# A fused add and GELU bound by its DMA queue: which load goes out first

## Chip, cores and metric

One core of a Trainium2 chip. The metric is the device time of one execution in microseconds (us); lower is better. Before: 120.17 us, median of 3 executions (120.11 to 120.28).

## The reference

```python
def setup_inputs():
    batch, dim = 1024, 4096
    return {"x": randn(batch, dim) as float32, "y": randn(batch, dim) as float32}

def reference(x, y):
    z = x + y
    return 0.5 * z * (1 + tanh(sqrt(2 / pi) * (z + 0.044715 * z ** 3)))
```

Two inputs of 16.8 MB are read and one output of 16.8 MB is written. Each byte crosses the memory once, 50.33 MB in all.

## The kernel before

A partition holds 32768 columns (8 whole rows). x is loaded straight into the tile of the sum, in two loads of 64 KB per partition. y comes in four loads of 32 KB per partition and has two buffers. The sum is made in chunks of 2048 columns by GpSimd or VectorE. ScalarE takes the absolute value and then the GELU of its negative, and VectorE finishes with max(z, 0) plus that.

```python
    YS = 8192
    xloads = [16384, 16384]
    yloads = [8192, 8192, 8192, 8192]
    FIRST = 8
    stores = [16384, 10240, 6144]
    by_dve = {0: 0, 2: 0, 4: 2, 6: 4, 8: 8, 12: 10}
    # ... pools: the tile of the sum once, y twice, PSUM work tiles twice ...

    sp = []
    for i, (a, b) in enumerate(xr):
        sp += [(load_x, i)] + [(load_y, j) for j, (c, _) in enumerate(yr) if a <= c < b]
    sp += [(store, i) for i in range(len(stores))]
    # ... VectorE: for each chunk c: the adds listed for c in by_dve, then end(c) ...
    # ... a manual schedule: each engine runs its list in order ...

    begin_early(nc, 2)    # the first two loads go ahead of the barrier at which the engines meet on entry
    wait_late(nc)
```

All loads and stores are issued by one engine (SP) onto one queue: x0, y0, y1, x1, y2, y3, then three stores. y2 must wait until y0's buffer is free, and the first store is held back until chunk 8 is half finished.

Of the kernel before, what the change touches and what calls it, by code (L numbers as in the profile page):

```python
# [66 lines left out]
def kernel(  # L67
# [33 lines left out]
    def ranges(sizes):  # L101
        ends = [sum(sizes[: i + 1]) for i in range(len(sizes))]
        assert ends[-1] == TOT
        return [(e - f, e) for e, f in zip(ends, sizes)]

    xr, yr, sr, cr = (ranges(r) for r in (xloads, yloads, stores, [CH] * (TOT // CH)))
# [63 lines left out]
            ends.setdefault(c, ins.ins)  # L170


    sp = []
    for i, (a, b) in enumerate(xr):
        sp += [(load_x, i)] + [(load_y, j) for j, (c, _) in enumerate(yr) if a <= c < b]
    sp += [(store, i) for i in range(len(stores))]
    pool = [(add, c) for c in range(C) if c not in by_dve]
    dve, acts = [], []
# [69 lines left out]
```

## Time and profile before

| | before |
|---|---|
| median | 120.17 us |
| span in the profile | 118.8 us |
| DMA queue busy | 98.5% |
| VectorE, ScalarE, GpSimd busy | 50%, 51%, 47% |
| first adds begin | 31.70 us |
| first store issued | 77.86 us |

Read the DMA share first: with the engines at 98.5%, only the moments when they have nothing to do can be gained. Those lie at the start and the end of the span. The lines themselves are in the prediction below; in them DVE is VectorE, ACT ScalarE, POOL GpSimd, and SPq the instructions by which SP issues transfers.

### The profile page before, as it was taken

How to read it: one execution, taken by the hardware profiler on the slowest of the kernel's cores; microseconds unless marked ns; L12 is line 12 of the kernel's file. 1: busy time of each engine (PE TensorE's matmuls, PEld its weight loads, DVE VectorE, ACT ScalarE, POOL GpSimd, SP SyncE). 2: the span in 40 equal slices, each digit the busy share in tenths (PEclk: the TensorE clock that was granted, in tenths of full speed). 3: DMA queues.
4: the chain of work that ended last, by engine and by line, in shares of the span. 5: the costliest groups of instructions: out<-in, count | busy, mean ns of one | idle time of the engine just before them, and what ended most of it. 6: DMA issues, size and time to landing. Idle time of an engine off the chain costs nothing.

```text
span 118.8 us, 160 instructions
## 1 busy us (share of the span) xinstructions
DVE 59.8 (50%) x24; ACT 60.8 (51%) x34; POOL 55.5 (47%) x14
## 2 busy tenths in 40 slices
DVE  0000000000399999699994595257999457742000
ACT  5000000000057989999369804797798999940000
POOL 0000000000399999998000029999999999200000
DMA  9899988989999988998899999998899889999895
GB/s 353 353 419 596 397 353 364 497 375 463 419 430 452 530 353 375 640 397 353 353 463 419 452 430 397 474 541 353 375 640 397 353 353 441 441 441 441 381 422 257
DMA packets 1296, 50.33 MB, mean 424 GB/s; under 512 B 144, under 2 KB 144, under 8 KB 144
## 3 DMA queue, kind: packets, MB, share of 16 engines
q1 hardware_dynamic: 1296, 50.33, 98.5%
HBM read 33.55 MB, written 16.78 MB: 424 GB/s over the span
## 4 chain that ended last, share of the span: by engine, by line
DMA 48%; POOL 33%; POOLq 4%; ACT 3%; DVE 2%; issue 0%; SPq 0%; DVEq 0%
DMA y<-in_y_dram 48%; POOL z L149 33%; POOLq L215 4%; DVE z L166 2%; ACT w L154 2%; ACT w L157 2%; SPq L125 0%; POOLq L149 0%; DVEq L166 0%
## 5 line engine op out<-in xcount | busy, mean ns | idle before, releaser
L149 POOL TENSOR_TENSOR z<-z,y 128x2048 f32<-128x2048 f32 x10 | 55.3, 5560 | 45.9 <-DMA y<-in_y_dram 45.9
L154 ACT ACTIVATE w<-z 128x2048 f32<-128x2048 f32 x16 | 30.1, 1880 | 42.8 <-DVE z L149 36.3
L166 DVE SCALAR_TENSOR_TENSOR z<-z,w 128x2048 f32<-128x2048 f32 (+1 forms) x17 | 36.3, 2156 | 16.0 <-ACT w L157 16.0
L149 DVE TENSOR_TENSOR z<-z,y 128x2048 f32<-128x2048 f32 x6 | 24.0, 4009 | 30.6 <-DMA y<-in_y_dram 30.6
L157 ACT ACTIVATE w<-w 128x2048 f32<-128x2048 f32 x16 | 29.8, 1862 | 0.5
L200 ACT ACT_TABLE_LOAD x1 | 1.3, 1283 | 1.3 <-PEq L232 1.3
L199 DVE MEMSET one<- 128x1 f32 x1 | 0.1, 59 | 1.3 <-PEq L232 1.3
L200 ACT ACTIVATE one<-one 128x1 f32<-128x1 f32 x1 | 0.2, 203 | 0.0
L232 POOL MEMSET const-float32-0.0<- 128x1 f32 x1 | 0.1, 99 | 0.2 <-issue 0.2
L232 POOL MEMSET const-bfloat16-1.0<- 128x1 bf16 x1 | 0.1, 102 | 0.0
L232 POOL MEMSET const-uint8-127<- 128x1 uint8 x1 | 0.1, 102 | 0.0
L232 POOL MEMSET const-float32-1.0<- 128x1 f32 x1 | 0.1, 99 | 0.0
## 6 DMA issues: line engine op xcount, KB each, us to landing
y<-in_y_dram SPq DMA_DIRECT2D x4, 4096.0 KB, 28.3
out_dram<-z SPq DMA_DIRECT2D x1, 5120.0 KB, 14.9
out_dram<-z SPq DMA_DIRECT2D x1, 3072.0 KB, 10.9
z<-in_x_dram SPq DMA_DIRECT2D x2, 40.5
out_dram<-z SPq DMA_DIRECT2D x1, 21.6
```

Of the source, the lines that this page charges most:

```text
L149: eng.tensor_add(out=zt[:, a:b], in0=zt[:, a:b], in1=yt[s][:, o : o + b - a])
L154: nc.scalar.activation(out=wt[c], in_=zt[:, a:b], func=act.Abs)
L157: nc.scalar.activation(out=wt[c], in_=wt[c], func=act.Gelu_apprx_tanh, scale=-1.0)
L166: ins = nc.vector.scalar_tensor_tensor(out=zt[:, a + o : a + o + n], in0=zt[:, a + o : a + o + n], scalar=0.0, in1=wt[c][:, o : o + n], op ...
L199: nc.vector.memset(one, 0.0)
L200: nc.scalar.activation(out=one, in_=one, func=act.Gelu_apprx_tanh)
L215: tc.compile()
L232: nc = _bacc.Bacc("TRN2", target_bir_lowering=False, num_devices=1)
```

## The change

The first load is to be a smaller one: y's first quarter, in rows of 32 KB, in place of x's first half in rows of 64 KB, which follows. The intent is a start that fills the DMA engines sooner. Nothing else changes.

```diff
-    sp = []
-    for i, (a, b) in enumerate(xr):
-        sp += [(load_x, i)] + [(load_y, j) for j, (c, _) in enumerate(yr) if a <= c < b]
+    sp = [(load_y, 0), (load_x, 0), (load_y, 1), (load_x, 1), (load_y, 2), (load_y, 3)]
     sp += [(store, i) for i in range(len(stores))]
```

## The prediction

> **What bounds the kernel now.** I read the page first: the slices, the DMA totals and the busy shares. Then I read the stretches of time cut at the borders of the transfers, the issue times of the load and store lines, the timeline of the queue's own engine, and last the chain of waits, to see whether it contradicts the rest.
>
> From the page:
>
> ```profile
> DVE 59.8 (50%) x24; ACT 60.8 (51%) x34; POOL 55.5 (47%) x14
> ...
> DMA  9899988989999988998899999998899889999895
> ...
> DMA packets 1296, 50.33 MB, mean 424 GB/s; under 512 B 144, under 2 KB 144, under 8 KB 144
> ...
> q1 hardware_dynamic: 1296, 50.33, 98.5%
> ```
>
> The compute engines are busy half of the time. The one DMA queue holds the 16 DMA engines for 98.5% of 118.8 us, 117.0 us, so only 1.8 us of the span has no transfer, as a mean over the engines. 1296 packets less the 144 tiny ones (9 transfers by 16, the completion marks) are 1152, 9 transfers by 128 rows: each row of a partition is one packet, 64 KB for x, 32 KB for y. In the whole run each engine moves 72 rows, 50.33 MB / 16 = 3.146 MB.
>
> Where the 1.8 us lies is told by stretches cut at the borders. The columns are the stretch, its length, the busy time of VectorE, ScalarE and GpSimd, the clock, the DMA share and GB/s. A packet is put down to the stretch in which it starts, so a short stretch can show a share over 1.
>
> ```profile
> 0.00:1.00 1.00, 0.00 (x0) 0.00 (x0) 0.20 (x4) 1.00 0.00 0
> 1.00:1.60 0.60, 0.06 (x1) 0.34 (x1) 0.00 (x0) 1.00 5.10 1748
> 1.60:3.80 2.20, 0.00 (x0) 1.14 (x2) 0.00 (x0) 1.00 0.00 0
> 3.80:4.70 0.90, 0.00 (x0) 0.00 (x0) 0.00 (x0) 1.00 2.69 1165
> ...
> 118.40:118.80 0.40, 0.00 (x0) 0.00 (x0) 0.00 (x0) 1.00 0.00 0
> ```
>
> No packet starts in the first 1.00 us. All first packets of x start between 1.00 and 1.60 (1748 GB/s for 0.60 us is 1.05 MB, 16 rows of 64 KB), and 5.10 x 0.60 = 3.06 us is their mean time. The second round, between 3.80 and 4.70, takes 2.69 x 0.90 = 2.42 us each. So the first packet of each engine costs 0.64 us more than the next. With the packets of the trace laid end to end on 16 engines I find no gap over 0.05 us on any of them until the end. The sum closes: 1.0 to 1.5 until the engines start, 0.64 of extra first packet, 3.146 MB at 64 KB per 2.42 us (27.1 GB/s per engine) = 116.2, about 0.4 after the last packet, together 118.2 to 118.7 against the span of 118.8.
>
> The queue's own engine and the chain:
>
> ```profile
> 0.00 0.38 SPq L125 DMA_DIRECT2D z<-in_x_dram  x1
> 0.43 1.16 SPq L132 DMA_DIRECT2D y<-in_y_dram  x2
> 1.64 0.50 SPq L125 DMA_DIRECT2D z<-in_x_dram  x1
> 44.92 13.59 SPq L132 DMA_DIRECT2D y<-in_y_dram  x2
> 77.86 30.28 SPq L136 DMA_DIRECT2D out_dram<-z  x3
> ```
>
> ```profile
> 0.43 31.17 DMA y<-in_y_dram
> ...
> 31.75 13.16 POOL z L149 x2
> ...
> 105.49 2.29 DVE z L166
> ```
>
> The chain gives 33% to GpSimd's adds, since it follows what released the last store. It is the chain of issues, not the bound: each issue comes while the queue still has work. By rows and rates y2 begins to move at about 59.5 us, 14.5 after its issue at 44.92; the first store at about 78.8, 0.97 after its issue at 77.86; the last at about 110.3, some 2.5 after its issue near 107.8. The first store is the close one: its lead is about the latency of an issue at the start (1.0 us to the first packet), and still no gap opens.
>
> **What the Trainium skill says.** "DMA: Bandwidth & Descriptors", section "Where 436 GB/s comes from", gives a ceiling of 435 GB/s for 16 ports; the steady packets run at 65,536 B / 2.42 us x 16 = 433 GB/s, so the trace agrees and nothing is left in the steady state. The same page, "Queues, rings and completion order", says that each DMA engine consumes its descriptors in ring order; the trace agrees (a landing per transfer in the order of issue), so a swap of two queued loads swaps no bytes past a third. Its "Latency and other measured facts" gives about 600 ns to the first byte for a transfer from this queue; here 1.0 us from the start of the issue, or 0.62 after its 0.38 us, which agrees if counted from the issue's end. No page tells why the first packet is 0.64 us longer, nor whether that grows with the row.
>
> **The change part by part.** Nothing is removed or added: the same nine transfers, rows and arithmetic, and the compiled instruction streams differ only in the first two entries of the queue's own engine, and in which of the two completion marks some waits name. Both first transfers still go out ahead of the entry barrier.
> - First issue. The first load is y0, not x0. The issues of x take 0.38 (first) and 0.50 us, those of y 0.33 three times and 0.42 once (right behind x). I take 0.33 to 0.38 for y as the first: a gain of 0 to 0.05 us, straight on the path, since the engines are empty until then.
> - First packet. If the 0.64 us is the filling of an empty pipe, it stays 0.64 on a row of 1.21 us (a first packet of about 1.85 us): no change. If it goes with the bytes of the first row (3.06 / 2.42 = 1.27 times), it is 0.32 and the run gains 0.32 us. I give the second a chance of one in five: 0.06 us as a mean.
> - Supply. Behind the first transfer the queue needs the second in time. y0 occupies each engine for 8 x 1.21 + 0.64 = 10.3 us instead of 20.0, and x0 is issued 0.4 us later. No gap.
> - First adds. Both y0 and x0 must be there, 12.6 MB: 8 x (2.42 + 1.21) us of rows either way. The adds start at 31.7 us as before, within a few tenths. The early y0 buys nothing, as no instruction can use y alone.
> - All that follows has the same order: y1, x1, y2, y3, stores. y2 needs y0's buffer free after the first four adds, which are not moved.
> - Sum: -0.05 to 0 for the issue, -0.06 for the first packet, 0 elsewhere: about -0.1 us of 120.17. The time outside the span (120.27 - 118.8 = 1.5 us in the profiled run) isn't touched.
>
> **Rivals.**
> - The startup is much better with 32 KB rows: the engines start within 0.5 us of each other, perhaps because a 64 KB row costs more to describe, and the whole extra 0.64 us of the first packet vanishes. For it: x's issues are the longest. Against it: the second x issue, 0.50 us, left no trace in the packets. At best it makes 120.17 - 0.64 - 0.3 = 119.2 us, 0.8%.
> - The last bytes before the first adds now come in 64 KB rows. The engines end such a row up to 0.7 us apart (first rounds spread over 0.8 us), and if the completion came later by half a row, 1.2 us, the adds and the issue of y2 would move by that. y2 has over 14 us to spare, so that is hidden. But the first store has about none: its issue hangs on an add of y2's data, which lands by the queue's pace and not by the early adds, so it doesn't move. If it slipped all the same, its delay is idle time of the engines: 120.2 plus the slip, some 0.2 to 1 us.
> - The compute becomes the bound at the end: the last store's issue stands about 1.5 us ahead of need (2.5 less the 1.0 of latency). All of ScalarE's chain from 70.5 us on starts from y2's landing, so it moves with the queue. A change of several us is needed to matter. It would have to come from a changed VectorE/GpSimd overlap, and nothing there is reordered.
>
> **Range and chances.** The point is 120.17 - 0.1 = 120.07, so about 120.05. The three runs of before lie within 0.17 us. Adding a full gain of the first-packet term (-0.32) below, and noise with a small slip of the first store above, gives 119.75 to 120.35. Two per cent is 2.4 us, more than the entire time outside steady transfer on the DMA engines; faster by that would need steady rates to change, slower a gap of 2.4 us in a queue that keeps its order. I give each 1%.
>
> **What would show it.** Right: DMA share again at 98 to 99%, the same 1296 packets, first packets starting about 0.95 to 1.0 us into the span, a mean of about 1.85 us for the first 16 rows (share times width of that stretch) and 1.21 for the next, the first adds at 31.5 to 31.8, no stretch without packets near the first store. The first-packet term is wrong if those rows take about 1.5 us, or if the second rows too are over 1.21. The whole is wrong if the first adds move by over 1 us, a hole opens ahead of a store, or the rate in the middle leaves 433 GB/s.

## The result, and the profile after

Ratios are the mean time of one kernel's runs over that of the other's runs of the same rounds, so they are not quite the ratio of the medians quoted. Executions over 1.5% slower than the fastest of the same kernel are left out of the means.

The first measurement: 120.06 us (120.00 to 120.10, 6 executions) against 120.22 for the kernel before (120.11 to 120.28, 6 executions); ratio 0.9986, 95% interval 0.9973 to 0.9999. That is within 2%, and at face value a gain of 0.16 us. Two later sets of rounds of the same kernel gave 0.9999 and 0.9999, so the experiments have to say whether that gain exists.

The page of the changed kernel (engines' busy time, DMA by slice, the queue):

```profile
DVE 59.8 (50%) x24; ACT 60.8 (51%) x34; POOL 55.5 (47%) x14
...
DMA  7989888998889988988899898998899889999996
...
q1 hardware_dynamic: 1296, 50.33, 98.6%
```

The same work, the same packets, the same share. The start, in stretches (columns as in the prediction):

```profile
0.00:1.00 1.00, 0.00 (x0) 0.00 (x0) 0.20 (x4) 1.00 0.00 0
1.00:2.30 1.30, 0.06 (x1) 1.04 (x1) 0.00 (x0) 1.00 1.26 403
2.30:2.70 0.40, 0.00 (x0) 0.39 (x2) 0.00 (x0) 1.00 0.00 0
2.70:3.30 0.60, 0.00 (x0) 0.06 (x1) 0.00 (x0) 1.00 2.04 874
...
118.10:118.60 0.50, 0.00 (x0) 0.00 (x0) 0.00 (x0) 1.00 0.00 0
```

Still no packet starts before 1.00 us. The first rows start between 1.00 and 2.30 (403 GB/s for 1.30 us is 0.52 MB, 16 rows of 32 KB) and last 1.26 x 1.30 = 1.64 us on average; the second rows last 2.04 x 0.60 = 1.22. So the first row costs about 0.43 us more than its bytes need, against 0.64 before. The last packet starts before 118.10 us.

The timeline of the queue's own engine, then the chain that ended last (both with start and duration in us, then what it was; pieces of one line that follow each other are merged, waits between them included):

```profile
0.00 0.38 SPq L132 DMA_DIRECT2D y<-in_y_dram  x1
0.43 0.42 SPq L125 DMA_DIRECT2D z<-in_x_dram  x1
1.26 0.33 SPq L132 DMA_DIRECT2D y<-in_y_dram  x1
1.64 0.45 SPq L125 DMA_DIRECT2D z<-in_x_dram  x1
44.68 13.59 SPq L132 DMA_DIRECT2D y<-in_y_dram  x2
77.61 30.28 SPq L136 DMA_DIRECT2D out_dram<-z  x3
```

```profile
0.43 30.92 DMA z<-in_x_dram
...
31.49 13.17 POOL z L149 x2
...
105.25 2.29 DVE z L166
```

The first issue takes 0.38 us, exactly as x's did. The load that comes last before the first adds is now x in place of y, and its piece is 0.25 us shorter (30.92 against 31.17); all other pieces have the same lengths within 0.02 us and stand 0.24 to 0.26 us earlier. The whole difference of these two traces was therefore made before 31.5 us, at the start.

Laying the packets of a trace end to end on 16 engines tells more. I call "begin" of an engine the end of its first row less the normal time of such a row (2.42 us for 64 KB, 1.21 for 32 KB). From there on each engine moves its 72 rows without a gap over 0.012 us in these two traces, so the slowest begin sets the end as long as the later rows keep their length. In the trace of before the begins have mean 1.84 and maximum 2.24 us, and the engines end at 117.95 on average and 118.33 at the slowest. In the changed kernel they begin at 1.80 on average and 1.95 at the slowest, and end at 117.94 and 118.06. **On average over the engines the two traces end at the same moment; only the slowest engine differs, by 0.27 us.** That gave Theory S: a 64 KB first row lets the engines spread further, a 32 KB row less. Rival T: it is y's tensor, not the row. Rival I: issues falling beside the first rows disturb them. Rival N: the spread is chance, different in each execution.

### The profile page after: what moved, and what is told of

The parts are those of the page before. It is cut to its first block, busy times and chain, and to the rows that moved or that the text cites. A ratio compares the mean times of both kernels' runs of the same rounds, so it can differ in the third digit from the quotient of the medians.

```text
span 118.6 us, 160 instructions
## 1 busy us (share of the span) xinstructions
DVE 59.8 (50%) x24; ACT 60.8 (51%) x34; POOL 55.5 (47%) x14
## 2 busy tenths in 40 slices
DMA packets 1296, 50.33 MB, mean 424 GB/s; under 512 B 144, under 2 KB 144, under 8 KB 144
## 3 DMA queue, kind: packets, MB, share of 16 engines
q1 hardware_dynamic: 1296, 50.33, 98.6%
## 4 chain that ended last, share of the span: by engine, by line
DMA 48%; POOL 34%; POOLq 4%; ACT 3%; DVE 2%; issue 0%; SPq 0%; DVEq 0%
POOL z L149 34%; DMA z<-in_x_dram 26%; DMA y<-in_y_dram 21%; POOLq L213 4%; DVE z L166 2%; ACT w L154 2%; ACT w L157 2%; SPq L132 0%; POOLq L149 0%; DVEq L166 0%
```

## The experiments

All kernels below computed the correct output. Each line gives the begins (mean and slowest), the excess of the first row (the time by which it is longer than normal, on average over the engines), and what the rounds said. "Disturbance" is the time by which the other rows were longer than normal, per engine on average. The sets of rounds ran on different chips (4, 15 and 0 in the record; the first set's is not recorded), so a kernel is compared with its own companions first.

### The changed kernel again (twice)

No edit.

> The changed kernel once more, unedited. Read from the two traces: on average over the 16 engines the last packet ends at the same moment in both kernels (117.95 and 117.94 us), but the slowest engine ends at 118.33 before and 118.06 after, since the engines leave the first row 0.80 us apart before and 0.40 after. Theory S (spread by the first row's size): this profile shows again a spread of the first rows' ends of 0.3 to 0.5 us, a span of 118.5 to 118.6, and 0.10 to 0.25 us less than the kernel before. Rival N (chance of one execution): the spread is 0.6 or more here, or the spans of the rounds overlap with those of the kernel before.

Measured: 120.14 us (119.99 to 120.63) against 120.31 (120.11 to 120.54), ratio 0.9999, interval 0.9980 to 1.0018. Begin 1.72, slowest 1.98, excess 0.60, span 118.55. The trace fits Theory S in its begins (first rows end 0.57 us apart, a little over the 0.3 to 0.5 expected), but the rounds overlap: two of the six executions took 120.6.

> The changed kernel for a third trace and a third set of rounds. In the traces so far the slowest engine begins at 2.24, 2.31, 2.09, 2.04 and 2.30 us where the first row has 64 KB and at 1.95, 1.98, 2.09 and 1.97 where it has 32 KB; the means over engines are 1.79 to 1.91 and 1.72 to 1.80. Theory S: 1.9 to 2.1 at the slowest and 1.70 to 1.80 on average here, ratio 0.998 to 1.000. Rival N: 2.2 or more at the slowest.

Measured, in the last set: 120.28 us (120.04 to 120.77) against 120.27 (120.15 to 120.51), ratio 0.9999, interval 0.9980 to 1.0018. In this trace the engines begin at 1.96 on average and **2.60 at the slowest**, later than in any trace of a 64 KB first row. Its stretches at the start:

```profile
1.00:2.30 1.30, 0.06 (x1) 1.04 (x1) 0.00 (x0) 1.00 1.57 403
...
2.70:3.30 0.60, 0.00 (x0) 0.06 (x1) 0.00 (x0) 1.00 1.96 710
3.30:3.80 0.50, 0.00 (x0) 0.00 (x0) 0.00 (x0) 1.00 0.32 131
```

The same 16 rows now last 1.57 x 1.30 = 2.04 us, 0.82 more than their bytes need, in place of 0.43, and second rows still start after 3.30 us, where the trace first shown had none. Same kernel, same stretch: the excess differs by 0.40 us between two executions, more than the whole difference that I had set out to explain. Rival N is what this run was written to detect, and it did.

### The kernel before again

No edit.

> The kernel before once more, for a second trace of it. Data of an engine can be said to begin at the end of its first row less the normal time of such a row; over the engines that moment was 1.84 us on average and 2.24 at the slowest before, 1.80 and 1.95 in the changed kernel, 1.72 and 1.98 in its repeat, 1.86 and 2.31 with the inputs exchanged. Theory S (64 KB rows leave the slowest engine later): here again 2.2 to 2.35 at the slowest and 1.80 to 1.90 on average. Rival N (chance of one execution): a slowest engine at 2.0 or less.

Measured: 120.23 us (120.12 to 120.32) against 120.16 (120.11 to 120.41), ratio 1.0002, interval 0.9989 to 1.0015. Begin 1.82, slowest 2.09, first row 2.30 x 1.30 = 2.99 us by this line, an excess of 0.57 (its first stretch with packets):

```profile
1.00:2.30 1.30, 0.06 (x1) 1.04 (x1) 0.00 (x0) 1.00 2.30 807
```

2.09 lies between the two expectations: less than Theory S asked for, more than Rival N did. Its span of 118.64 is 0.15 us under the first trace of the same kernel.

### The inputs exchanged: y first, but in rows of 64 KB

```diff
-        tile_add_gelu_kernel(tc, *args)
+        tile_add_gelu_kernel(tc, args[1], args[0], args[2])
```

> The kernel before with the two inputs exchanged (a sum does not care): the first load is y, in rows of 64 KB, into the tile of the sum. Theory S (row size): as the kernel before, span 118.8, ratio 1.000, first rows' ends 0.7 to 0.9 us apart. Rival T (it is y's tensor or its place in HBM that starts more evenly): as the changed kernel, span 118.55, ratio 0.9985, ends 0.4 apart.

Measured: 120.36 us (120.28 to 120.63) against 120.31, ratio 1.0011, interval 0.9998 to 1.0024. Begin 1.86, slowest 2.31, excess 0.69, span 118.9, of which 0.28 us is disturbance between 40 and 79 us. In this one trace it is as the kernel before, not as the changed one, and nothing speaks for Rival T. Since two traces of one kernel differ by as much, one trace does not exclude it.

### x first, but in rows of 32 KB

```diff
-    xloads = [16384, 16384]
+    xloads = [8192, 8192, 16384]
...
+    sp = [(load_x, 0), (load_x, 1), (load_y, 0), (load_y, 1), (load_x, 2), (load_y, 2), (load_y, 3)]
```

> x first, as before, but its first half in two loads with rows of 32 KB; one transfer more (10). Theory S (row size): as the changed kernel, first rows' ends 0.3 to 0.5 us apart, span 118.55 to 118.65 (0.03 of it for 8 more packets per engine), ratio 0.9985. Rival T (tensor): as the kernel before, 0.7 to 0.9 apart, span 118.8. My prediction's two readings of the first packet: a constant fill gives an excess of 0.64 us on the first row, one that goes with bytes 0.32; the changed kernel showed 0.43.

Measured: 120.24 us (120.04 to 120.96) against 120.31, ratio 1.0006, interval 0.9983 to 1.0029. Begin 1.76, slowest 2.09, excess 0.51, first rows end 0.51 apart, disturbance in the middle 0.21. The first rows look like those of the changed kernel; the time can't tell the two theories apart.

### y first in rows of 16 KB, and in rows of 4 KB

```diff
-    yloads = [8192, 8192, 8192, 8192]
+    yloads = [4096, 4096, 8192, 8192, 8192]        # 16 KB; for 4 KB: [1024, 7168, 8192, 8192, 8192]
...
+    sp = [(load_y, 0), (load_x, 0), (load_y, 1), (load_y, 2), (load_x, 1), (load_y, 3), (load_y, 4)]
```

> The changed kernel with y's first quarter cut in two loads with rows of 16 KB, the first ahead of x, the second behind it. Theory S, if the spread goes on halving with the row: first rows' ends 0.2 us apart and the span 118.45, 0.1 under the changed kernel. If the spread has a floor (the engines receive their first packet up to 0.9 us apart), it stays at 0.4 or is larger, since a late engine is no longer made up for, and the span is 118.6 or more. Excess of the first row: 0.43 if constant, 0.2 if it goes with the bytes.

Measured: 120.12 us (120.09 to 120.31, 5 executions) against 120.31, ratio 0.9990, interval 0.9977 to 1.0002. Excess of the first row about 0.54 us on 0.61 us of transfer; span 118.6. A fast engine's second row starts before a slow one's first here, and with 4 KB, so first rows can't be told from second ones by their start. The completion marks settle it: each engine moves a packet of 4 B behind its eight rows of a load, and the start of that packet, less eight normal rows, gives the begin of every engine. By the marks the begins are 1.79 on average and 1.98 at the slowest, 0.32 us apart. The first trace of the changed kernel has 0.40 by the same reckoning and its second 0.58, so the spread is neither halved again nor larger; one trace can't say more.

> The changed kernel with a small first load: y's first 1024 columns, rows of 4 KB, then x's first half, then the remaining 28 KB rows of that quarter. If the excess at the start is a constant filling of each engine, the first rows still last about 0.55 us more than their bytes need, and the slowest engine begins by 1.9 to 2.1 us, span 118.5 to 118.65 without disturbance in the middle. If it goes with the bytes of the first row, it falls to 0.05 and moves to the 64 KB rows behind it. If a small first row helps further than 32 KB did, the slowest is at 1.8 or less and the span 118.4.

Measured: 120.34 us (120.21 to 120.38, 5 executions) against 120.27, ratio 1.0000, interval 0.9989 to 1.0012. Excess about 0.4 us on a row of 0.16 us, and 0.50 over the eight rows of an engine. By the completion marks the begins are 1.81 on average, as with long rows, and 2.22 at the slowest, outside the 1.9 to 2.1 expected of a constant filling. The span of 118.9, over the range expected too, is that late engine: only 0.07 us of disturbance lies between 40 and 79 us. A small first row did not bring the engines closer together (0.55 us apart).

Together these settle what the excess is not. By row size the first-row excess is: 64 KB 0.64, 0.57, 0.69, 0.63, 0.61; 32 KB 0.43, 0.60, 0.82, 0.51, 0.59, 0.69; 16 KB 0.54; 4 KB about 0.4 (0.50 over eight rows). A sixteenth of the bytes leaves over half of the excess: it does not go with the bytes. Nor is it a fixed price that each engine pays. In the first trace of the changed kernel the three engines whose first packet starts by 1.04 us have an excess of 0.53 to 0.92, and the two that start last, at 1.90 and 1.95, have none. What stays is the begin: by the marks its mean is 1.73 to 1.89 us in twelve of the thirteen traces, whatever the row. The thirteenth is the third trace of the changed kernel, with 2.21, since there the rows behind the first lost another 0.25 us.

### The third load issued late

```diff
     def load_y(i):
         ...
+        if i == 1:
+            tc.add_manual_dep(ins, <first load>.name, DependencyInfo(Sync, DATA))
```

> The kernel before, but the third load (and so all later ones) is issued only when the first has landed, at about 22 us, so that no issue falls beside the first rows (before, issues ran at 1.26 and 1.64 us while the first rows moved from 1.0 to 4.7). Rival I (those issues disturb the first rows): the excess of the first row falls from 0.64 us to 0.4 or less and the slowest begins by 2.0, span 118.5. Theory S says the row alone does it: excess 0.6 to 0.7, slowest 2.2 to 2.35, span as before; the queue has 10 us of y's rows left at the issue, so no gap.

Measured, on the kernel before: 120.36 us (120.16 to 120.67) against 120.16, ratio 1.0014, interval 0.9999 to 1.0029. The issue did move, to about 22 us, as the timeline of the queue's own engine shows (the second line's 21.63 us hold the wait):

```profile
0.00 0.37 SPq L125 DMA_DIRECT2D z<-in_x_dram  x1
0.42 21.63 SPq L132 DMA_DIRECT2D y<-in_y_dram  x2
22.11 0.42 SPq L125 DMA_DIRECT2D z<-in_x_dram  x1
```

Begin 1.79, slowest 2.04, excess 0.63. The excess stays, so Rival I fails for the third load and those behind it; the slowest engine, though, is at 2.04 where Theory S asked for 2.2. The span of this trace is 119.1 all the same: 0.64 us of disturbance lies between 40 and 79 us. A startup that was 0.2 us better than in the first trace was lost three times over in the middle.

> The same in the changed kernel: the third load waits until the first has landed, at 12 us, with 20 us of x's rows left in the queue. Rival I: excess under 0.3, slowest begins by 1.8, span 118.3. Theory S: as the changed kernel, excess 0.4 to 0.6, slowest 1.9 to 2.1, span 118.55 plus noise.

Measured, on the changed kernel: 120.09 us (120.05 to 120.23, 5 executions) against 120.16, ratio 0.9991, interval 0.9979 to 1.0003. Begin 1.74, slowest 1.97, excess 0.59, span 118.7 with 0.23 of disturbance. No gain from the late issue either.

### Only one load ahead of the barrier

```diff
-    begin_early(nc, 2)
+    begin_early(nc, 1)
```

> The kernel before with only x's load ahead of the entry barrier; y's first load is issued behind it, at about 0.9 to 1.3 us in place of 0.43. If the second issue, which lies between the first issue and its first packet, delays or spreads the first packets (Rival I in its second form), the first packets start earlier than 1.0 us or the excess falls by 0.2 or more. Theory S: start 1.0, excess 0.6 to 0.7, slowest 2.2 to 2.35, ratio 1.000.

Measured: 120.22 us (120.13 to 120.52, 5 executions) against 120.16, ratio 1.0003, interval 0.9991 to 1.0015. y's first load was issued at 0.79 us in place of 0.43. First packets at 1.02, begin 1.91, slowest 2.30, excess 0.61, span 119.0 with 0.31 of disturbance between 40 and 79 us. Moving the second issue by 0.36 us changed nothing at the start. But it ran from 0.79 to 1.12 us, so it still lay beside the first packets; no run here has a start without a second issue, and Rival I in this form is not excluded.

### An order that is not free: y0 and y1 ahead of x

```diff
-    sp = [(load_y, 0), (load_x, 0), (load_y, 1), (load_x, 1), (load_y, 2), (load_y, 3)]
+    sp = [(load_y, 0), (load_y, 1), (load_x, 0), (load_x, 1), (load_y, 2), (load_y, 3)]
```

> The changed kernel with y's second quarter ahead of x too: y0, y1, x0, x1, y2, y3. The bytes, rows and buffers are the same, only the moment at which the first pair is complete moves, from 31.4 to about 41.1 us. If the order of the loads were free as long as the DMA engines have work (Rival: only the byte total counts), the time stays at 120.1. My reading of the margins says not: the adds, ScalarE's chain of 8 chunks (33.8 us from its first piece to the end of the eighth) and the last finishing piece ahead of the first store move by about 9.7 us, less what the wait for y2 near 70.4 absorbs. ScalarE's eighth chunk ends at 77.5 and the first store is issued at about 82.5 in place of 77.6; it is needed about 1 us before 78.8. So a hole of 4 to 5 us opens in the queue, and the time is 124 to 125.5 us, ratio 1.03 to 1.045.

Measured: 132.76 us median of 4 executions (128.96 to 132.98) against 120.27. Three of the four, the profiled one among them, count as slow because they exceed the fastest by more than 1.5% (at a clock of 1.00, as in the fastest), so no ratio is given; but the fastest, 128.96, too is 8.7 us above the kernel before. In the profile the DMA engines stand still for about 12.6 us each ahead of the first store. The page (each digit a slice of 3.3 us), the chain that ended last, and the stores in the timeline of the queue's own engine:

```profile
DMA  9899989977977977979999790002979779999997
...
q1 hardware_dynamic: 1296, 50.33, 89.4%
```

```profile
1.25 39.84 DMA z<-in_x_dram
...
77.40 0.06 DVE z L166
77.46 2.15 issue
79.61 6.33 DVE z L149
85.96 1.89 ACT w L154
```

```profile
91.01 30.18 SPq L136 DMA_DIRECT2D out_dram<-z  x3
```

The first pair is complete at 41.1 us, as expected, and ScalarE's eighth chunk ends at 77.3 (expected 77.5). My estimate failed after that: the ninth chunk's add stands in VectorE's own order behind the finishing piece of the eighth, so it began at 79.61 and not at y2's landing near 70.3. There it met GpSimd's adds, under way since 70.31, and took 6.33 us. In the kernel before, VectorE's add of that chunk started at 70.48, just ahead of GpSimd's at 70.53, and took 2.29. The Trainium skill, "SBUF — State Buffer", section "Who interferes with whom", says that a VectorE instruction with two SBUF inputs contends with GpSimd instructions that read SBUF, and that the order of issue decides who blocks; the two durations agree with it. So do the ends: the GpSimd add that was under way at 79.61 ended at 83.78, and VectorE's ended 2.14 us later, about the 2.29 us that it takes when it goes first. In the kernel before it was GpSimd's add that was longer, 6.62 us beside VectorE's and 4.52 for the next one. That one execution took 3.8 us less would fit a 2.3 us add in place of a 6.3 us one, but there is no trace of it, so this is only argued.

So the order of queued loads is not free in general. The one exchange that kept the moment at which a pair is complete cost nothing measurable; the one order that moved it by 9.7 us cost 8.7 us or more.

### What all of it says on the small gain

Begins of the engines, mean and slowest, one trace each:

| first row | traces | mean | slowest |
|---|---|---|---|
| 64 KB | 5 | 1.84, 1.82, 1.86, 1.79, 1.91 | 2.24, 2.09, 2.31, 2.04, 2.30 |
| 32 KB | 6 | 1.80, 1.72, 1.96, 1.76, 1.74, 1.80 | 1.95, 1.98, 2.60, 2.09, 1.97, 2.02 |
| 16 KB (by the marks) | 1 | 1.79 | 1.98 |
| 4 KB (by the marks) | 1 | 1.81 | 2.22 |

Order for 64 KB: before, again, inputs exchanged, late third load, one early. For 32 KB: changed, its second and third trace, x in 32 KB, late third load, y0 and y1 first.

Five of six slowest begins of the 32 KB kernels lie at or under 2.09, three of five of the 64 KB kernels over 2.2; the sixth, 2.60, is the latest of all, and the 4 KB row is late too. Over the three sets of the changed kernel, 18 executions have median 120.09 and mean 120.22 us; 44 executions of the kernel before (its companions in those three sets and in one more, and its own repeat) have 120.245 and 120.26. The means differ by 0.04 us with a standard error of 0.06 (the spread of single executions over the root of their number, both kernels together). Set by set, against its own companions, the changed kernel's mean is 0.17 us lower, 0.03 lower and 0.06 higher. So the typical execution may be some 0.15 us shorter, and a share of the executions (5 of 18 at 120.44 or more, against 3 of 44) is longer and takes it back; neither is settled. No kernel here is shown to beat the kernel before.

## Why the prediction was right

- **The bound.** Right: the DMA queue at 98.5 and 98.6%, no hole over 0.012 us on an engine, the same 1296 packets. That is why exchanging two loads changed next to nothing. Its point of 120.05 against 120.06 measured is closer than it deserves: later sets gave medians of 120.14 and 120.28, with the kernel before at 120.31 and 120.27. That was luck: in the two profiled traces neither of the two terms of its -0.1 us made the difference, but the slowest engine, which it had left out.
- **First issue.** It allowed a gain of 0 to 0.05 us; y's issue took 0.38 us, as x's had. The gain was zero, and so was that of the first packet's time (1.0 us in every trace).
- **First packet.** The likelier reading was right in that the excess does not go with the bytes: it is 0.43 to 0.82 us from 64 down to 16 KB. It was wrong in its picture of a fixed 0.64 us per engine, since engines with a late first packet have less or none. Its figure of 1.85 us for the first row met 1.64, 1.81 (0.60 + 1.21) and 2.04; the first of these, taken alone, stands nearer to the rejected reading (about 1.5). The term of -0.06 us, the chance-weighted gain if the excess went with the bytes, should have been 0, and the 4 KB rows show it.
- **What it left out.** It worked with the mean over the engines, while the slowest engine sets the end. The first two traces differ by 0.27 us there and by 0.01 on average.
- **First adds.** Expected within 31.5 to 31.8 us, measured 31.45, just outside: the 0.25 us of the slowest engine again.
- **First store.** No hole opened; its issue moved with the loads, 77.86 to 77.61 us, as argued. That the margin there does not bear a late pair is what y0 and y1 ahead of x showed.
- **The range.** It held all six executions of the first measurement, but only 13 of all 18: single executions of either kernel scatter further than the three that I had. One sum of the prediction is off: by its own figures the time outside steady transfer is 118.8 - 116.2 = 2.6 us, not under 2.4. Nearly all of it would have had to go for 2%, so the low chance stands.

## What to carry to other kernels

Where one DMA queue is full from end to end, exchanging two queued loads whose data are used together moved nothing here that three sets of rounds could tell from noise; ask instead whether any reorder delays the moment at which a pair is complete, since that costs as soon as the compute behind it no longer reaches the stores in time. Read the start per engine, not on average, as the slowest engine ended the run in the two traces compared. And before explaining a difference of 0.1% from two traces, take a second trace of the same kernel: here two executions of one kernel differed more than the two kernels did.

## What the Trainium skill lacked or had wrong

- "DMA: Bandwidth & Descriptors", section "Latency and other measured facts", has the first-byte latency of about 600 ns (here the earliest packet started 1.00 to 1.02 us after the start of the issue in every trace, 0.62 to 0.65 after its end), but not that the first row of most engines then lasts longer than its bytes need: 0.4 to 0.8 us on average over the engines, not proportional to the row from 4 to 64 KB, and up to 1.6 us on one engine.
- "SBUF — State Buffer", section "The DMA setup-cost knee", gives a fixed cost of about 2 us per transfer. In a queue that is never empty none of it shows between transfers: gaps of at most 0.012 us in both kernels, over nine transfers of 3 to 8 MB. Only the start (1.8 us until an engine begins, on average) and the end (about 0.5 us after the last packet) pay.
- No page tells that load rows lengthen in some executions and not in others: between 40 and 79 us from 0.03 to 0.64 us per engine in total, over traces whose loads there are nearly the same and at full clock. The kernel with 0.64 scattered from 118.7 to 119.2 us of span by itself. What disturbs the loads is open; no run here separates it.
- "DMA: Bandwidth & Descriptors", section "Where 436 GB/s comes from", from which the prediction took the 435 GB/s, goes on to say that for transfers between HBM and SBUF an HBM limit of about 358 GB/s per core binds. With one core at work that limit did not show: the load rows ran at 433 GB/s over all engines, and the mean over the whole span was 424.
